# An encoder block on one core: five of the eight column groups of the gate projections by seven half-sized block products, in a stage of their own behind the local attention

## The chip, the cores and the metric

The kernel runs on one core of one Trainium2 chip. The metric is the device time in microseconds (us) of one execution; lower is better. Engines are named as the profile names them: PE (TensorE matmul), PEld (its weight load), DVE (VectorE), ACT (ScalarE), POOL (GpSimd), SP (SyncE, which issues nearly all DMAs here, in order, each after the waits that it carries).

## The reference

One layer of an encoder with 512 tokens and width 2048, all in float32:

```python
mod = silu(c) @ w_ada + b_ada                      # shift, scale, gate for both halves
h   = rms_norm(x) * (1 + sc1) + sh1
qa, ka, va, qb, kb, vb, ga, gb = split(h @ w_in)   # ga, gb: 2048 columns each
ya  = global_gqa(rope(norm(qa)), rope(norm(ka)), va)   # 8 heads, all 512 keys
yb  = neighbourhood_attention(qb, kb, vb, nat_rpb)     # 8 heads, 8x16 windows
m   = sigmoid(ga) * (ya @ w_oa) + sigmoid(gb) * (yb @ w_ob)
x   = x + g1 * (m @ w_out)
h2  = rms_norm(x) * (1 + sc2) + sh2
x   = x + g2 * ((silu(h2 @ w_ffn_gate) * (h2 @ w_ffn_up)) @ w_ffn_down)
out = rms_norm(x)
```

## The kernel before

Every product is made of three float32r matmuls (`mm3`): each operand is split into a high part (ACT copy, `whi`, `..h`) and a low part (DVE or POOL subtraction, `wlo`, `..l`), and high*high, high*low and low*high are summed in PSUM. Weights come in units of 512 KB by SP into the tile `raw` (four buffers), are split into `whi` and `wlo` (three buffers each), and are used once.

Two forms of product are used for the projections. `form1` makes two tiles of 128 output columns over the 16 tiles of the width, tokens along the free axis: 16 x 2 x 3 = 96 matmuls of 512 columns. `form2` makes 512 output columns with tokens on the partitions: 192 such matmuls. In the feed-forward part `group7` makes 512 columns by seven block products of a 2 x 2 blocking (Winograd's variant of Strassen's scheme): for each of four steps over the width, `wforms` loads two units, forms the sums of weight blocks `ta` (DVE) and `tb` (POOL) and splits four tiles; then each of seven products takes 12 matmuls of 256 columns, 84 a step, 336 a group. `xforms` does the same once for the moving operand. Seven DVE additions (lines 765 to 771) put the products together at the end of a group. There the pools have five buffers of `raw` and of the split weights.

The stages, in the order of the program:

1. The first 228 us: norm of x, the modulation `ada1`, h (`hT`, 16 pairs of tiles that stay in SBUF until the gates are done), k and v, the first half of q, the first four column tiles of `ga`.
2. Global attention (`att_a`): four heads, the second half of q (`form2`), `ga` 4 to 8 (`gates`, two `form1`), four heads, `ga` 8 to 16 (four `form1`).
3. Local attention, two halves of four heads: v of the half by `form2` straight into its split tiles (line 572), then twice q and k of two heads (`form1`) and `att_b` for both.
4. `gb` 0 to 16: eight `form1`, each result copied and stored to DRAM (`keep_gate`).
5. The 16 attention results `y_d` are read back (`yr`, in the buffers of `raw`) and split into `yT`; then `w_oa`, `w_ob` with the gates read back; then `w_out`; then the feed-forward part.

Beside the stages runs a queue `bg` of generators, one step of which (`pump`) is taken after each unit of weights: `ada_mod` (eight generators, the second modulation) from stage 3 on, then `ada_gate` (eight generators, two gate rows); a step loads 512 KB of `w_ada` into a `raw` buffer and adds it up with two DVE instructions (line 257).

A scheduler puts each engine's instructions in a fixed order: it follows the program, but moves work of a later statement ahead where an earlier one still waits and buffers are free. So the matmuls of the next `form1` or `form2` stand among those of the heads. A pool that is released and allocated anew sets a limit to this: what lies in the new one waits for what lay there before. The weight pools `wp` and `io` live from the start to the end of `w_ob`.

Of the kernel before, what the change touches and what calls it, by code (L numbers as in the profile page):

```python
# [80 lines left out]
def encoder_block(ctx: ExitStack, tc, xp, c, w_ada, b_ada, norm1_w, w_in, q_norm_w, k_norm_w, tb,  # L81
# [197 lines left out]
    def ada_gate(col, q, dst):  # L279
# [6 lines left out]
        y = bank("Y")  # L286
# [111 lines left out]
    def keep_gate(dst):  # L398
        def evac(w, j, b):
            o = io.tile([P, T], F32, tag="go", name="go", bufs=2)  # L400
# [104 lines left out]
    for h in range(4):  # L505
        att_a(h, q, h, 0)
    q1 = [st(F32) for _ in range(NT)]
# [9 lines left out]
    gates(sg_a, GA, 8, 16, G)  # L517
# [62 lines left out]

    bg.extend(ada_gate(2 * D, q, g1_d) for q in range(4))
    bg.extend(ada_gate(5 * D, q, g2_d) for q in range(4))
    gates(sg_b, GB, 0, KT)
    p_b.release()
    p_h.release()

# [89 lines left out]
    ORDER = (1, 2, 3, 5, 6, 7, 4)  # L676
    HALVES = ((1,), (2, 3), (5, 6), (7, 4)), ((1,), (2, 4), (5, 6), (7, 3))
    BANK = {1: "mm", 2: "mm", 3: "mm", 5: "mm", 6: "S", 7: "S", 4: "Y"}

    def form_pool(name, side):  # L680
        return tc.alloc_tile_pool(name=name, bufs=1, side=side, reuse_waits="tile")

    def half(t, n=2):
        return t.rearrange("p (a q n) -> p a q n", q=2, n=256) if n == 2 else t.rearrange("p (q n) -> p q n", q=2)

    def split7(parts, tiles, kinds):

        d = {}
        for (src, views), (hi, lo), rs in zip(parts, tiles, kinds):
            split(hi, lo, src)  # L690
            for r, v in zip(rs, views):
                d[r] = (v(hi), v(lo))
        return d

    def wforms(w, k0, c0):
        rt = []
        for a in range(2):
            raw, r3 = unit(w, k0 + 2 * a, 2, c0, 512)
            rt.append((raw, r3[:, :, :256], r3[:, :, 256:]))
        (_, b11, b12), (r1, b21, b22) = rt  # L700
        ta = wp.tile([P, 1024], F32, tag="ta", name="ta", bufs=2)
        tb = wp.tile([P, 1024], F32, tag="tb", name="tb", bufs=1)
        t1, t2_ = (half(ta)[:, a] for a in range(2))
        t3, t4 = (half(tb)[:, a] for a in range(2))
        V.tensor_sub(t1, b12, b11)
        V.tensor_sub(t2_, b22, t1)
        G.tensor_sub(t3, b22, b12)  # L707
        G.tensor_sub(t4, t2_, b21)  # L708
        hl = [[wtile(t) for t in ("whi", "wlo")] for _ in range(4)]
        col = lambda e: lambda t: t.rearrange("p (q n) -> p q n", q=2)[:, :, e * 256:(e + 1) * 256]  # L710
        blk = lambda e: lambda t: half(t)[:, e]
        g0 = [t[:, :512].rearrange("p (q n) -> p q n", q=2) for t in hl[0]]
        return split7(((b11, (lambda t: t,)), (r1, (col(0), col(1))), (ta, (blk(0), blk(1))), (tb, (blk(0), blk(1)))),
                      [g0] + hl[1:], HALVES[0])

    def xforms(pool, e, o, full=False):

        sa = wp.tile([P, 1024], F32, tag="ta", name="sa", bufs=2)
        sb = wp.tile([P, 1024], F32, tag="tb", name="sb", bufs=1)
        a11, a21 = e[:, :512], e[:, 512:]  # L720
        a12, a22 = o[:, :512], o[:, 512:]
        V.tensor_add(sa[:, :512], a21, a22)
        V.tensor_sub(sa[:, 512:], sa[:, :512], a11)
        G.tensor_sub(sb[:, :512], a11, a21)
        G.tensor_sub(sb[:, 512:], a12, sa[:, 512:])
        tl = [[pool.tile([P, 512 if n == 0 else 1024], F32R, tag=f"x{n}{t}", name=f"x{n}{t}") for t in "hl"]
              for n in range(4)]
        blk = lambda n: lambda t: t[:, n * 512:(n + 1) * 512].rearrange("p (q n) -> p q n", q=2)
        d = {}
        if full:  # L730
            h21 = [wtile(t)[:, :512] for t in ("whi", "wlo")]
            split(*tl[0], a11)
            split(*h21, a21)
            split(*tl[1], o)
            d["21"] = tuple(blk(0)(t) for t in h21)
            for n, rs in ((0, (1,)), (1, (2, 4))):
                for j, r in enumerate(rs):
                    d[r] = tuple(blk(j)(t) for t in tl[n])
            d.update(split7(((sa, (blk(0), blk(1))), (sb, (blk(0), blk(1)))), tl[2:], HALVES[1][2:]))
            return d  # L740
        return split7(((a11, (blk(0),)), (o, (blk(0), blk(1))), (sa, (blk(0), blk(1))), (sb, (blk(0), blk(1)))),
                      tl, HALVES[1])

    at7 = iter((4, 8, 12, 16, 20, 24, 28, 32, 36, 40, 44, 48, 52, 56, 60, 0, 1, 2, 56, 24, 40))

    def group7(wsrc, xs, order, dst):

        wbufs["at"] = next(at7)
        bk = {r: bank(BANK[r]) for r in ORDER}
        for n, s in enumerate(order):  # L750
            w = wsrc(s)
            for r in ORDER:
                (wh, wl), (xh, xl) = w[r], xs[s][r]
                for q in range(2):
                    for c in range(2):
                        o = bk[r][:, c * 256:(c + 1) * 256]
                        cs = slice(c * P, (c + 1) * P)
                        first, last = n == 0 and q == 0 and c == 0, n == len(order) - 1 and q == 1
                        mm3(o, wh[:, q, cs], wl[:, q, cs], xh[:, q], xl[:, q], first, last, skip_group_check=True)
        p = {r: b.rearrange("p (c n) -> p c n", c=2) for r, b in bk.items()}  # L760
        (d11, d12), (d21, d22) = dst
        with tc.high_priority():
            p1 = io.tile([P, 512], F32, tag="io", name="p1").rearrange("p (c n) -> p c n", c=2)
            S.activation(p1, p[1], AF.Copy)
            V.tensor_add(d11, p[2], p1)
            V.tensor_add(d21, p[6], p1)
            V.tensor_add(d12, p[5], d21)
            V.tensor_add(d12, p[3], d12)
            V.tensor_add(d21, p[7], d21)
            V.tensor_add(d22, p[5], d21)  # L770
            V.tensor_sub(d21, d21, p[4])

# [188 lines left out]
```

## Time and profile before

| | |
|---|---|
| median of 3 runs | 2812.9 us (2806.91, 2812.9, 2821.86) |
| span of the profiled execution | 2800.4 us (its own time is not listed apart) |
| PE busy | 2672.3 us, 95% of the span |
| DVE, ACT, POOL busy | 1730.4, 961.7, 617.0 us |
| moved by DMA | 427.17 MB, mean 153 GB/s |
| global attention and what stands beside it | about 228 to 497 us |
| local attention | about 497 to 818 us |
| `gb` | from about 793 us, beside the last two heads, to 986 us |
| `w_oa` and `w_ob`, `w_out` | 992 to 1171 us, 1175 to 1368 us |
| feed-forward, first part (21 `group7`) and second part | to about 2285 us, to 2800 us |

"Span" runs from the first to the last instruction; a run's time has some us more around it. Busy shares of PE are modelled, so the distance between the starts of two matmuls says more on its pace than the busy time.

### The profile page before, as it was taken

How to read it: one execution, taken by the hardware profiler on the slowest of the kernel's cores; microseconds unless marked ns; L12 is line 12 of the kernel's file. 1: busy time of each engine (PE TensorE's matmuls, PEld its weight loads, DVE VectorE, ACT ScalarE, POOL GpSimd, SP SyncE). 2: the span in 40 equal slices, each digit the busy share in tenths (PEclk: the TensorE clock that was granted, in tenths of full speed). 3: DMA queues.
4: the chain of work that ended last, by engine and by line, in shares of the span. 5: the costliest groups of instructions: out<-in, count | busy, mean ns of one | idle time of the engine just before them, and what ended most of it. 6: DMA issues, size and time to landing. Idle time of an engine off the chain costs nothing.

```text
span 2800.4 us, 38853 instructions
## 1 busy us (share of the span) xinstructions
PE 2672.3 (95%) x15353; PEld 2331.3 (83%) x15353; DVE 1730.4 (62%) x2277; ACT 961.7 (34%) x1310; POOL 617.0 (22%) x366
## 2 busy tenths in 40 slices
PE   5888999999999999899899999999999989999998
PEld 4676878788887878677789999999999988878886
DVE  8987461566665566565568877777788753243227
ACT  4224441233331233222544444444444433122122
POOL 2544323000100000011123443333434410011000
PEclk8889999999999999999989999999999999999999
DMA  8772224655556577676333343334333354343232
GB/s 256 255 235 83 83 68 153 193 157 168 173 168 198 186 254 249 221 260 199 95 113 121 122 128 118 116 108 130 126 119 120 125 192 163 97 143 120 90 113 83
DMA packets 281238, 427.17 MB, mean 153 GB/s; under 512 B 16992, under 2 KB 148432, under 8 KB 278496
## 3 DMA queue, kind: packets, MB, share of 16 engines
q1 hardware_dynamic: 280720, 423.59, 46.9%
q8 instruction: 120, 1.97, 0.3%
q10 hardware_dynamic: 336, 1.11, 0.1%
q14 instruction: 62, 0.51, 0.1%
HBM read 392.11 MB, written 32.52 MB: 152 GB/s over the span
## 4 chain that ended last, share of the span: by engine, by line
PE 77%; DVE 10%; DMA 8%; ACT 2%; issue 2%; SPq 0%; POOL 0%; DVEq 0%; ACTq 0%
PE mm L122 19%; PE mm L124 19%; PE mm L123 19%; DMA raw<-in_w_ada 6%; DVE acc L257 5%; PE S L122 3%; PE S L123 3%; PE S L124 3%; PE Y L122 2%; PE Y L123 2%; PE Y L124 2%; DMA ffr<-ffd 1%; ACT whi L114 1%; PE T L494 1%; DVE wlo L115 0%
## 5 line engine op out<-in xcount | busy, mean ns | idle before, releaser
L114 ACT ACTIVATE whi<-raw 128x1024 fp32r<-128x1024 f32 (+1 forms) x466 | 455.2, 978 | 1077.0 <-PE mm L124 404.8
L115 DVE TENSOR_TENSOR wlo<-raw,whi 128x1024 fp32r<-128x1024 f32 (+1 forms) x408 | 499.4, 1227 | 494.6 <-ACT whi L114 489.7
L257 DVE SCALAR_TENSOR_TENSOR acc<-raw,cact,acc 128x512 f32<-128x512 f32 (+1 forms) x383 | 324.9, 851 | 138.0 <-DMA raw<-in_w_ada 129.0
L707 POOL TENSOR_TENSOR tb<-raw 128x512 f32<-128x512 f32 x84 | 116.0, 1380 | 505.6 <-DVE wlo L115 497.8
L115 POOL TENSOR_TENSOR wlo<-raw,whi 128x1024 fp32r<-128x1024 f32 (+1 forms) x58 | 142.7, 2465 | 236.5 <-ACT whi L114 204.9
L115 DVE TENSOR_TENSOR wlo<-ta,whi 128x1024 fp32r<-128x1024 f32 x84 | 129.4, 1541 | 70.5 <-ACT whi L114 70.1
L708 POOL TENSOR_TENSOR tb<-ta,raw 128x512 f32<-128x512 f32 x84 | 145.1, 1727 | 0.0
L646 POOL TENSOR_TENSOR xr<-xr,ro 128x512 f32<-128x512 f32 x32 | 49.3, 1572 | 434.0 <-DVE ro L645 434.0
L114 ACT ACTIVATE whi<-ta 128x1024 fp32r<-128x1024 f32 x84 | 89.2, 1062 | 142.1 <-PE mm L123 142.1
L114 ACT ACTIVATE whi<-tb 128x1024 fp32r<-128x1024 f32 x84 | 89.1, 1061 | 133.4 <-PE S L123 119.9
L123 PE MATMUL mm<-x1l,whi 128*128 128x256 f32 x400 | 112.4, 281 | 0.0
L122 PE MATMUL mm<-x1h,whi 128*128 128x256 f32 x400 | 112.3, 281 | 0.0
L124 PE MATMUL mm<-x1h,wlo 128*128 128x256 f32 x400 | 112.3, 281 | 0.0
L115 DVE TENSOR_TENSOR wlo<-tb,whi 128x1024 fp32r<-128x1024 f32 x84 | 102.5, 1221 | 10.0 <-ACT whi L114 8.3
L122 PE MATMUL mm<-x0h,whi 128*128 128x256 f32 x368 | 104.5, 285 | 3.3 <-ACT whi L114 3.3
L124 PE MATMUL mm<-x0h,wlo 128*128 128x256 f32 x368 | 104.4, 284 | 0.8 <-DVE wlo L115 0.8
L123 PE MATMUL mm<-x0l,whi 128*128 128x256 f32 x368 | 104.5, 284 | 0.0
L250 POOL MEMSET acc<- 128x512 f32 x8 | 4.2, 526 | 427.9 <-DVE ada_s L115 158.6
L123 PE MATMUL mm<-x3l,whi 128*128 128x256 f32 x336 | 94.3, 281 | 0.0
L123 PE MATMUL S<-x2l,whi 128*128 128x256 f32 x336 | 94.3, 281 | 0.0
L123 PE MATMUL S<-x3l,whi 128*128 128x256 f32 x336 | 94.3, 281 | 0.0
L123 PE MATMUL mm<-x2l,whi 128*128 128x256 f32 x336 | 94.3, 281 | 0.0
(1311 smaller groups left out, 8242.9 us busy)
## 6 DMA issues: line engine op xcount, KB each, us to landing
raw<-in_w_in SPq DMA_DIRECT2D x134, 512.0 KB
raw<-in_w_ada SPq DMA_DIRECT2D x256, 256.0 KB
raw<-in_w_gate SPq DMA_DIRECT2D x88, 512.0 KB
raw<-in_w_up SPq DMA_DIRECT2D x88, 512.0 KB
raw<-in_w_down SPq DMA_DIRECT2D x88, 512.0 KB
raw<-in_w_ada SPq DMA_DIRECT2D x64, 512.0 KB
raw<-in_w_out SPq DMA_DIRECT2D x40, 512.0 KB
ffr<-ffd SPq DMA_DIRECT2D x22, 512.0 KB
```

The costliest lines, as they stand in the source:

```text
L114: S.activation(hi, src, AF.Copy)
L115: eng.tensor_sub(lo, src, hi)
L122: nc.tensor.matmul(o, lh, rh, start=start, stop=False, **kw)
L123: nc.tensor.matmul(o, lh, rl, start=False, stop=False, **kw)
L124: nc.tensor.matmul(o, ll, rh, start=False, stop=stop, **kw)
L250: G.memset(acc, 0.0)
L257: V.scalar_tensor_tensor(acc, part, cact[:, k:k + 1], acc, op0=ALU.mult, op1=ALU.add)
L494: nc.tensor.transpose(tp[:, k * P:(k + 1) * P], e[:, k * P:(k + 1) * P], ident)
L646: eng.tensor_add(x2[i][:, cs], x2[i][:, cs], o)
L707: G.tensor_sub(t3, b22, b12)
L708: G.tensor_sub(t4, t2_, b21)
```

## The change

- `ada_mod` joins the queue already behind the first four heads of the global attention; it was ahead of the local attention.
- `ga` 8 to 16 leave their place behind the global attention. There v of both halves of the local attention is made now (`form2`), copied from PSUM and stored to DRAM (`vbd`); at the start of each half it is read back (`vr`, in the buffers of `raw`) and split.
- Behind the last head all that is left of `bg` is run to its end (`settle`); `p_b`, `io` and `wp` are released, and a stage of its own begins with pools `wg`, `iog` (`raw` four buffers, split weights three) and `p_s`. It makes `gb` 0 to 4 by two pairs of `form1` as before. Beside them `hforms` forms the sums of blocks of h (POOL adds high and low part into `eo`, in buffers of `raw`; DVE forms `sa`, `sb`; 8 splits in all). Three of the seven products need no new tile: a small class `Block` hands out slices of `hT`.
- Then five `group7` of 512 columns: `gb` 4 to 16 and `ga` 8 to 16, results by way of the tile `c` to DRAM. `group7` takes a `pump` per step now. `ada_gate` runs in this stage and goes on in `w_oa`; its small product lies in bank "T" instead of "Y".
- At the end one `settle`, release of the four pools, new pools `wo` and `ioo`, and the code from `gpool` on as before. The definitions of `group7`, `wforms` and the rest are moved ahead, unchanged.

```diff
+    def settle():
+        if bg:
+            for _ in bg.pop(0):
+                pass
...
     for h in range(4):
         att_a(h, q, h, 0)
+    bg.extend(ada_mod(3 * D, 4 * D, k, 2, (s2, b_sc2, n2, t2, b_sh2)) for k in range(0, KT, 2))
...
-    gates(sg_a, GA, 8, 16, G)
+    vb_d = [[dram.tile([P, T], F32, name=f"vbd{h}{i}") for i in range(NT)] for h in range(2)]
+    for h in range(2):
+        form2(w_in, VB + h * 512, hT, lambda i, b: keep_gate(vb_d[h])(0, i, b), eng=G)
...
-    bg.extend(ada_mod(3 * D, 4 * D, k, 2, (s2, b_sc2, n2, t2, b_sh2)) for k in range(0, KT, 2))
     for half in range(2):
         v = [pair(p_b, "v", 512, NT) for _ in range(NT)]
-        form2(w_in, VB + half * 512, hT, lambda i, b: split(*v[i], b))
+        for i in range(NT):
+            vr = wp.tile([P, 1024], F32, tag="raw", name="vr", bufs=4)[:, :512]
+            nc.sync.dma_start(vr, vb_d[half][i])
+            split(*v[i], vr)
...
-    bg.extend(ada_gate(2 * D, q, g1_d) for q in range(4))
-    bg.extend(ada_gate(5 * D, q, g2_d) for q in range(4))
-    gates(sg_b, GB, 0, KT)
+    while bg:
+        settle()
     p_b.release()
+    io.release()
+    wp.release()
...
+    wp = tc.alloc_tile_pool(name="wg", bufs=1, side="right", reuse_waits="tile")
+    io = tc.alloc_tile_pool(name="iog", bufs=3, side="right", reuse_waits="tile")
+    bg.extend(ada_gate(2 * D, q, g1_d) for q in range(4))
+    bg.extend(ada_gate(5 * D, q, g2_d) for q in range(4))
+    p_s = form_pool("p_s", "right")
...
+    def hforms(s):
+        eo = []
+        for a in range(2):
+            r = wp.tile([P, 1024], F32, tag="raw", name="eo", bufs=wbufs["raw"])
+            for q in range(2):
+                hi, lo = (t.rearrange("p (t n) -> p t n", t=2) for t in hT[4 * s + 2 * a + q])
+                G.tensor_add(half(r)[:, :, q], hi, lo)
+            eo.append(r)
+        (a11, a21), (a12, a22) = ((r[:, :512], r[:, 512:]) for r in eo)
+        sa = wp.tile([P, 1024], F32, tag="ta", name="sa", bufs=2)
+        sb = wp.tile([P, 1024], F32, tag="tb", name="sb", bufs=1)
+        V.tensor_add(sa[:, :512], a21, a22)
+        V.tensor_sub(sa[:, 512:], sa[:, :512], a11)
+        V.tensor_sub(sb[:, :512], a11, a21)
+        V.tensor_sub(sb[:, 512:], a12, sa[:, 512:])
...
+    for j in range(0, 4, 2):
+        form1([w_in], GB + j * P, 2, hT, [[bank("mm"), bank("mm")]], keep_gate(sg_b[j:], "io", 3))
+        gx += [hforms(j), hforms(j + 1)]
+    for base, dst, j0, j1 in ((GB, sg_b, 4, KT), (GA, sg_a, 8, KT)):
+        for j in range(j0, j1, 4):
+            c = io.tile([P, 2048], F32, tag="c", name="c", bufs=1)
...
+            group7(lambda s: wforms(w_in, 4 * s, base + j * P), gx, range(4),
+                   ((v[:, 0, 0], v[:, 1, 0]), (v[:, 0, 1], v[:, 1, 1])), 16)
...
+    settle()
+    p_s.release()
+    io.release()
+    wp.release()
     p_h.release()
+    wp = tc.alloc_tile_pool(name="wo", bufs=1, side="right", reuse_waits="tile")
+    io = tc.alloc_tile_pool(name="ioo", bufs=3, side="right", reuse_waits="tile")
```

Three places show how the order of instructions moves. In the rows, a name left of the arrow is written, names right of it are read; `mm`, `S`, `T`, `Y` are PSUM banks; line numbers after the change are higher by some lines.

PE before, at the first scores of heads 2 and 3 of the local attention (`S<-qk..`); `mm<-whi,h0h` is the next dense product, v of the second half:

```order
L124 MATMUL mm<-h15h,wlo 128x512
L122 MATMUL mm<-whi,h0h 128x512
L122 MATMUL S<-qkh 128x256
L122 MATMUL S<-qkh 128x384
L123 MATMUL mm<-wlo,h0h 128x512
L124 MATMUL mm<-whi,h0l 128x512
L123 MATMUL S<-qkl,qkh 128x256
L124 MATMUL S<-qkh,qkl 128x256
L123 MATMUL S<-qkl,qkh 128x384
L124 MATMUL S<-qkh,qkl 128x384
```

PE now, from the last part of the same two heads (`T<-ident,e` transposes, `Y<-pt..` the weighted sums) to the first dense product behind them, q of the second half:

```order
L124 MATMUL Y<-pth,vl 128x256
L564 MATMUL T<-ident,e 128x128 x8
L122 MATMUL Y<-pth,vh 128x384
L564 MATMUL T<-ident,e 128x128 x2
L123 MATMUL Y<-ptl,vh 128x384
L124 MATMUL Y<-pth,vl 128x384
L122 MATMUL Y<-pth,vh 128x256
L123 MATMUL Y<-ptl,vh 128x256
L124 MATMUL Y<-pth,vl 128x256
L122 MATMUL mm<-h0h,whi 128x512
```

From the first scores of heads 2 and 3 to their last sum no `mm` row stands on PE any more; the same holds for heads 6 and 7.

SP now, around the reading back of v for the second half (`vr`), ahead of the weights of q (`raw<-in_w_in`); `y_1975`, `y_1976` are the results of heads 2 and 3, `braw` the tables of the bias:

```order
L471 DMA y_1974<-yo 128x512
L581 DMA vr<-vbd_3593 128x512
L539 DMA braw<-in_tb 8x720 x16
L581 DMA vr<-vbd_3594 128x512
L581 DMA vr<-vbd_3595 128x512
L581 DMA vr<-vbd_3596 128x512
L539 DMA braw<-in_tb 8x720 x16
L471 DMA y_1975<-yo 128x512
L539 DMA braw<-in_tb 8x720 x4
L129 DMA raw<-in_w_in 128x4x256
L471 DMA y_1976<-yo 128x512
```

The four `vr` hold all four `raw` buffers; the first weights of q behind them wait until DVE has split the first, which in turn waits for the last sums of head 3, since the tiles of v are the same ones.

SP before, where the attention results are read back (`yr<-y`), ahead of the last stores of `gb` (`sgb_427`, `sgb_428`, its last two tiles):

```order
L597 DMA yr<-y_1965 128x512
L597 DMA yr<-y_1966 128x512
L402 DMA sgb_425<-go 128x512
L597 DMA yr<-y_1967 128x512
L402 DMA sgb_426<-go 128x512
L597 DMA yr<-y_1968 128x512
...
L597 DMA yr<-y_1980 128x512
L129 DMA raw<-in_w_oa 128x4x256 x2
L242 DMA raw<-in_w_ada 128x2x512
L129 DMA raw<-in_w_ob 128x4x256
L402 DMA sgb_427<-go 128x512
```

SP now, at the same place; `sga_411` to `sga_410` are the results of the last `group7`, `gate<-g1d` waits for PE's last read of `hT`:

```order
L247 DMA raw<-in_w_ada 128x2x512 x5
L301 DMA gate_9331<-g1d_4202 128x512
L764 DMA yr<-y_1965 128x512
L764 DMA yr<-y_1966 128x512
L764 DMA yr<-y_1967 128x512
L744 DMA sga_411<-c 256x1x256
...
L744 DMA sga_410<-c 256x1x256
L296 DMA g1d_4205<-ada_o 1x512
L764 DMA yr<-y_1968 128x512
...
L764 DMA yr<-y_1980 128x512
L301 DMA gate_9331<-g1d_4204 128x512
L129 DMA raw<-in_w_oa 128x4x256
```

Before, all 16 results are read back ahead of the stores of the last two tiles of `gb`. Now 13 of the 16 stand behind the results of the last `group7`, and the first weights of `w_oa` behind all 16.

More of the change, by code (lines that the diff above doesn't have):

```diff
@@ L285, in ada_gate @@
         split(hi, lo, acc)
-        y = bank("Y")
+        y = bank("T")
         nc.tensor.matmul(y, ones_r, hi, start=True, stop=False)
@@ L396, in encoder_block, with keep_gate @@
     p_x.release()
-    def keep_gate(dst):
+    def keep_gate(dst, tag="go", bufs=2):
         def evac(w, j, b):
-            o = io.tile([P, T], F32, tag="go", name="go", bufs=2)
+            o = io.tile([P, T], F32, tag=tag, name="go", bufs=bufs)
             V.tensor_copy(o, b)
@@ L671, in encoder_block @@
     gpool.release()
[L676 to L742, printed above, removed]
@@ L744, in encoder_block @@
-    at7 = iter((4, 8, 12, 16, 20, 24, 28, 32, 36, 40, 44, 48, 52, 56, 60, 0, 1, 2, 56, 24, 40))
[L746 to L771, printed above, removed]
@@ L834, in encoder_block @@
             dst = (v[:, 0, 0], v[:, 1, 0]), (v[:, 0, 1], v[:, 1, 1])
-            group7(lambda s: wforms(w, 4 * s, n * 512), hx, range(SU), dst)
+            group7(lambda s: wforms(w, 4 * s, n * 512), hx, range(SU), dst, next(at7))
             if w is w_gate:
```

108 lines of the change are left out of this document (107 added, 1 removed).

## The prediction

> **What bounds the kernel now.** I read the page first, then the busy time by stage, then the starts of single matmuls.
>
> ```profile
> span 2800.4 us, 38853 instructions
> PE 2672.3 (95%) x15353; PEld 2331.3 (83%) x15353; DVE 1730.4 (62%) x2277; ACT 961.7 (34%) x1310; POOL 617.0 (22%) x366
> 820.00:997.00 177.00, 168.97 (x730) 138.30 (x729) 92.26 (x116) 41.98 (x47) 1.52 (x3) 0.97 0.63 199
> 1620.00:1740.00 120.00, 120.00 (x1008) 120.00 (x1008) 94.18 (x93) 48.93 (x53) 47.64 (x28) 1.00 0.37 119
> ```
>
> Behind the stretch and its length stand the busy times of PE, PEld, DVE, ACT and POOL, then the granted clock, the DMA share and GB/s. PE bounds nearly everywhere: in the gates (820 to 997) and in the feed-forward block products (1620 to 1740), which run without a stall. DVE is busy there 94.18 of 120 us, so it has 21% left.
>
> **What a block product is worth.** In order of start, duration:
>
> ```profile
> 825.78 0.39 PE L122 MATMUL mm<-h0h,whi 128*128 128x512 f32 x1
> ...
> 847.54 0.39 PE L122 MATMUL mm<-h0h,whi 128*128 128x512 f32 x1
> 1692.21 0.28 PE L122 MATMUL S<-x3h,whi 128*128 128x256 f32 x1
> ...
> 1702.29 0.29 PE L122 MATMUL S<-x3h,whi 128*128 128x256 f32 x1
> ```
>
> The first two rows are the starts of two neighbouring `form1`: 96 matmuls of 512 columns in 21.76 us, 227 ns each. The other two are one step of `group7` apart: 84 matmuls of 256 columns in 10.08 us, 120 ns each. So half the columns cost 53% of the time. A group costs 2 x 21.76 = 43.5 us before and 4 x 10.08 = 40.3 now: five groups save 16 us on PE, not the eighth of 218 us (27) that counting columns gives. The Trainium skill (TensorE: Matmul & The Clock Gate, Back-to-back issue gap) gives N/2.4 + 2.5 ns for a warm matmul; estimated from it a group falls from 41.4 to 36.7 us, the five save 24 and the sum below would be 8 us lower. The rows here differ (227 and 120 ns against 216 and 109), so they decide.
>
> **Term 1, heads 2 and 3 without cover: +11.** In the new order PE has no dense product between the first scores and the last sum of these heads. Before, such a pair ran like this (start and end; stretch; then DVE over all four pairs of the stage, count, busy, mean ns):
>
> ```profile
> 792.80 0.51 PE L122 MATMUL S<-qkh 128*128 128x256 f32 x2
> ...
> 817.65 0.28 PE L124 MATMUL Y<-pth,vl 128*128 128x256 f32 x1
> 792.80:818.00 25.20, 25.20 (x134) 20.60 (x134) 22.21 (x59) 11.80 (x30) 0.00 (x0) 1.00 0.44 134
> L115 DVE TENSOR_TENSOR ptl<-T,pth 128x256 fp32r<-128x256 f32 (+1 forms) x32 | 15.6, 488 | 4.7 <-ACT pth L114 4.4
> L552 DVE SCALAR_TENSOR_TENSOR sb<-S,bm 128x256 f32<-128x256 f32 (+1 forms) x32 | 15.1, 479 | 0.1
> L471 DVE TENSOR_REDUCE mx<-sb 128x1 f32<-128x256 f32 (+1 forms) x32 | 14.8, 471 | 0.1
> L478 DVE TENSOR_SCALAR e<-e,rs 128x256 f32<-128x256 f32 (+1 forms) x32 | 12.7, 402 | 0.0
> L477 DVE RECIPROCAL rs<-sm 128x1 f32<-128x1 f32 x32 | 4.8, 155 | 0.6 <-ACT e L475 0.5
> L472 DVE TENSOR_SCALAR mx<-mx 128x1 f32<-128x1 f32 x32 | 4.6, 145 | 0.1
> L257 DVE SCALAR_TENSOR_TENSOR acc<-raw,cact,acc 128x512 f32<-128x512 f32 x83 | 63.5, 765 | 31.7 <-DMA raw<-in_w_ada 30.5
> ```
>
> PE was full for all 25 us. The pair's own part of it is 48 products of 256 or 384 columns at 0.12 to 0.17 us and 20 transposes at most as long as a 256: about 9 us. What remains alone is a chain over DVE: 67.6 / 4 = 16.9 us a pair by these rows, and the way through ACT and PE for the first and last block. Bounds of the chain: 13 us if durations overlap by a fifth, 25 as before. I take 20, nearer the DVE rows: PE idles 20 - 9 = 11 (4 to 16).
>
> **Term 2, v read back: +9.** Then q of the second half waits for a split of v (0.6 on ACT and 0.69 on DVE for 128x512), a transfer of 512 KB and a split of the weights. The nearest rows are the crossing from the gates to `w_oa`:
>
> ```profile
> 986.20 0.39 PE L124 MATMUL mm<-h15h,wlo 128*128 128x512 f32 x1
> 991.60 0.54 PE L122 MATMUL mm<-y0h,whi 128*128 128x512 f32 x1 [5.01 <-issue]
> 995.42 0.39 PE L124 MATMUL mm<-y1h,wlo 128*128 128x512 f32 x1
> 985.50 4.83 DMA raw<-in_w_oa
> 990.44 1.06 ACT whi L114
> 992.00:996.00 4.00, 3.76 (x11) 2.58 (x10) 3.08 (x4) 2.09 (x2) 0.00 (x0) 0.59 0.81 297
> L114 ACT ACTIVATE vh<-mm x8: 598/598/600, 536.0 to 694.2; 128x512 fp32r<-128x512 f32 x8
> L115 DVE TENSOR_TENSOR vl<-mm,vh x8: 679/686/692, 537.6 to 694.8; 128x512 fp32r<-128x512 f32 x8
> ```
>
> 4.83 us of transfer and 1.06 us of split stand ahead of the first matmul; behind it nine took 3.8 us where 2.0 would do, at a granted clock of 0.59: +1.8. So 1.3 + 4.8 + 1.1 + 1.8 = 9 (6 to 11, with or without the slow start and a prefetch).
>
> **Term 3, heads 6 and 7 without cover: +16.** As term 1, but `settle` puts ten of `ada_mod`'s DVE additions among the heads (0.77 us each in the last row of term 1, some waiting for their transfer behind the 16 of `braw`): 5 us more than term 1 (8 to 25).
>
> **Term 4, start of the gates' own stage: +9.** The first weights of `gb` stand on SP behind the store of head 7's result, so nothing is prefetched: copy 0.6, transfer 4.8, split 1.1, slow start 1.8 (6 to 12).
>
> **Term 5, end of that stage: +26.** Before, the 16 `yr` ran beside the last gates:
>
> ```profile
> 969.02 15.89 SPq L597 DMA_DIRECT2D yr<-y  x13
> L768 DVE TENSOR_TENSOR c<-mm,c 128x512 f32<-128x512 f32 x21 | 14.5, 691 | 0.7
> L115 DVE TENSOR_TENSOR wlo<-raw,whi 128x1024 fp32r<-128x1024 f32 (+1 forms) x408 | 499.4, 1227 | 494.6 <-ACT whi L114 489.7
> L257 DVE SCALAR_TENSOR_TENSOR acc<-raw,cact,acc 128x512 f32<-128x512 f32 (+1 forms) x383 | 324.9, 851 | 138.0 <-DMA raw<-in_w_ada 129.0
> 818.59 2.77 DMA y<-yo
> ```
>
> 13 issues in 15.89 us, 1.22 us each, paced by four buffers. Now they begin when PE is done with `hT`, and their splits when `c` is stored. From PE's last matmul: copy and seven additions 0.6 + 7 x 0.69 = 5.4; some of the last `ada_gate` additions between them, 3; store 2.8; four splits 2.8; nine more `yr` until a buffer is free for `w_oa`, 11; transfer and split 5.9. That is 31 us, less the 5.4 us of the same gap before (986.20 to 991.60): +26 (19, if splits don't wait for the store, to 35).
>
> **Term 6, DVE in the new stage: +5.** A step needs 94.18 / 120 x 10.08 = 7.9 us of DVE as in the feed-forward part, and two additions of `ada_gate`, 1.7: 9.6 of 10.08. With three buffers of split weights instead of five a late DVE stops PE soon. `hforms` (16 operations of 0.7, 8 splits of 1.2) beside two `form1` pairs, 16 additions and 8 splits comes to about 46 us of DVE in 43.5. I take 1 us a group (0 to 20 for all).
>
> **At nothing.** The cover of what moves ahead is the full PE of the global attention:
>
> ```profile
> 228.00:342.00 114.00, 102.84 (x511) 82.53 (x510) 71.86 (x158) 48.44 (x114) 39.74 (x22) 0.96 0.23 73
> 342.00:402.00 60.00, 56.24 (x282) 44.13 (x281) 33.32 (x72) 22.95 (x41) 20.18 (x10) 1.00 0.29 92
> ```
>
> v instead of `ga` 8 to 16 beside heads 4 to 7: 2 x 192 matmuls for 4 x 96. Eight copies, stores, reads and splits more: 0.7 us each on DVE beside a full PE; uncovered they would cost 6. `ada_mod` moved ahead: 128 additions beside the global attention, where DVE was busy 63% and 56% and the DMA share 0.23 and 0.29; where it delays a head's chain, up to 10. `ada_gate` leaving `w_out` may give back 2.
>
> **Sum**: -16 + 11 + 9 + 16 + 9 + 26 + 5 = +60 on the span of 2800.4 us. The runs lie 6 to 21 us above that span, the median 12.5; so 2812.9 + 60 = 2873.
>
> A stretch like the two uncovered pairs has one near relation, the crossing into the feed-forward part, with PE 72% busy:
>
> ```profile
> 1370.00:1425.00 55.00, 39.61 (x264) 36.05 (x265) 34.40 (x46) 35.67 (x47) 12.63 (x8) 0.79 0.20 64
> ```
>
> The granted clock is 0.79 there. At half clock the pair's products would lengthen each block's chain by some 0.6 us, 5 us a pair: 2883, inside the forecast. The same page of the Trainium skill (Part 1: The HAM clock gate) states half clock after an idle window of about 3.4 us, which this row neither excludes nor shows for matmuls spread thinly.
>
> **Rivals.**
> - *The crossings are covered after all*: pools with tile-wise waits let weights come early and the heads' chains run at 13 us. For it: PE's gap at 986 was only 5.4 us. Against: SP's order holds `raw` behind the last store in all three. Terms 1 to 5 then take their lower ends, 4 + 6 + 8 + 6 + 19: +27 with no stall in the new stage, 2840.
> - *DVE becomes the bound of the new stage*: POOL beside it and waits for `w_ada` make a step 11 us. 20 steps at 0.9 more, and 5 for the forms, make 23 to 25 instead of 5: 2893. The point is 10.08 us; 9.6 by the rows speaks slightly against.
> - *Faster, the block products alone decide*: the uncovered stretches come to little, since PE needs no cover that the heads' other engines don't bound: -16, 2797. It decides where terms 1 to 6 stay under 16 us together; term 5 alone exceeds that by the rows.
> - *No effect*: the stretches cost about what the products save, 2815.
>
> **How the numbers follow.** Two measurements of this kernel can be told apart from about 0.5%, 14 us. Chances: forecast (2850 to 2885) 0.58, covered crossings 0.17, DVE bound 0.12, faster 0.07, no effect 0.06. Slower is the sum of the first three, 0.87; same 0.06; faster 0.07. The range goes from the covered case less what the lowest run lies under the median (2840 - 6) to a bound DVE with what the highest lies above it (2893 + 9); it leaves out the last two and the tails.
>
> **What would show it.** Term 1 and 3: two stretches near 25 us of local attention with PE half idle and no `mm` row. Terms 2 and 4: PE waits of 6 to 8 us for `whi`, ended by a transfer of `w_in`. Term 5: a PE gap near 30 us ahead of the first `y0h` matmul. Term 6: steps of `group7` over 10.08 us, waits of PE for `wlo`. The saving: 120 ns between starts in the new stage. I am wrong if these gaps are absent, or if the steps are far from 10.08 us.

## The result and the profile after

The changed kernel takes 2920.5 us (median of 4 runs, 2913.7 to 2923.8) against 2811.4 for the kernel before on the same chip: ratio 1.0389, 95% interval [1.0374, 1.0405]. It is slower, as forecast, but 47 us beyond the forecast of 2873 and 18 above the upper end of the range, 2902. The profiled execution took 2913.7 us, its span is 2911.9: 111.5 more than before.

First lines of the page after:

```profile
span 2911.9 us, 40705 instructions
PE 2688.9 (92%) x16073; PEld 2365.9 (81%) x16073; DVE 1865.7 (64%) x2404; ACT 1008.1 (35%) x1363; POOL 706.2 (24%) x422
```

PE's busy time grew by 17 us, the span by 111.5: most of the time is in waits. Busy time by stretch (columns as in the prediction), of heads 2 and 3, of heads 6 and 7, of the last four `group7`, and of the piece from `ga` 4 to 8 to the local attention (first after the change, then before it):

```profile
616.00:642.00 26.00, 19.24 (x69) 14.60 (x68) 17.55 (x52) 10.80 (x29) 2.43 (x3) 0.59 0.05 14
752.80:777.50 24.70, 14.86 (x69) 10.75 (x68) 22.00 (x60) 9.50 (x26) 0.00 (x0) 0.86 0.10 33
895.50:1075.50 180.00, 164.26 (x1350) 159.60 (x1348) 151.02 (x161) 62.18 (x68) 49.02 (x31) 0.98 0.53 164
366.10:516.60 150.50, 132.09 (x631) 104.93 (x629) 82.17 (x154) 44.83 (x77) 39.84 (x19) 0.95 0.48 149
365.10:491.40 126.30, 121.80 (x607) 98.00 (x606) 58.47 (x118) 42.55 (x73) 38.85 (x19) 1.00 0.36 116
```

The two stretches of heads, in which PE was full before, have it at 19 of 26 and 15 of 25 us, the first at a granted clock of 0.59, the second at 0.86. In the last two rows 384 dense products of 512 columns stand beside heads 4 to 7 each time; after the change PE is idle there for 18.4 us instead of 4.5.

The matmuls that bound the pieces (start, duration; in brackets PE's idle time before and what ended it): first v product and first score of head 4; first q product of the local attention; both crossings between its halves; starts of the first, second and last `group7`; the end of the stage. The second and third row are DVE's, ahead of that first score: an addition of `ada_mod` that waits for its transfer, and `ql`, for which PE then waits.

```profile
366.08 0.48 PE L122 MATMUL mm<-whi,h0h 128*128 128x512 f32 x1
370.13 1.54 DVE L262 SCALAR_TENSOR_TENSOR acc<-raw,cact,acc 128x512 f32<-128x512 f32 x2 [5.67 <-DMA raw<-in_w_ada]
373.45 0.68 DVE L115 TENSOR_TENSOR ql<-T,qh 128x512 fp32r<-128x512 f32 x1
374.19 0.79 PE L124 MATMUL S<-kh,ql 128*128 128x512 f32 x1 [5.87 <-DVE ql L115]
516.60 0.63 PE L122 MATMUL mm<-h0h,whi 128*128 128x512 f32 x1
616.05 0.56 PE L122 MATMUL S<-qkh 128*128 128x256 f32 x2
645.82 0.79 PE L122 MATMUL mm<-h0h,whi 128*128 128x512 f32 x1 [3.46 <-ACT whi L114]
697.87 0.39 PE L122 MATMUL mm<-h0h,whi 128*128 128x512 f32 x1
752.84 0.56 PE L122 MATMUL S<-qkh 128*128 128x256 f32 x2
785.35 0.79 PE L122 MATMUL mm<-h0h,whi 128*128 128x512 f32 x1 [4.90 <-ACT whi L114]
840.77 0.39 PE L122 MATMUL mm<-h0h,whi 128*128 128x256 f32 x1 [2.48 <-ACT whi L114]
895.53 0.28 PE L122 MATMUL mm<-h0h,whi 128*128 128x256 f32 x1
...
1031.54 0.28 PE L122 MATMUL mm<-h0h,whi 128*128 128x256 f32 x1
1075.45 0.28 PE L124 MATMUL Y<-h15h,wlo 128*128 128x256 f32 x1
1107.89 0.76 PE L122 MATMUL mm<-y0h,whi 128*128 128x512 f32 x1 [27.14 <-ACT whi L114]
```

The groups take 54.8 us (the first) and 44 to 46 (the others, 180.2 in all) where 40.3 was the pace; before them the two `form1` take 55.4 where 43.5 was. What DVE waits for in the last four groups (total us, times, longest), and where the chain that ended last spends that stretch:

```profile
DVE acc L262 <- DMA raw<-in_w_ada: 14.7, 8, 2.7
DVE ta L627 <- DMA raw<-in_w_in: 12.5, 9, 4.1
by line: DVE wlo L115 18.7%; issue 16.3%; DMA raw<-in_w_in 13.7%; DMA raw<-in_w_ada 12.1%; DVE acc L262 8.6%; PE mm L124 3.2%; PE mm L122 2.7%; PE mm L123 2.6%; DVE ta L626 2.3%; POOL tb L628 1.6%; DVE ta L627 1.6%; DVE c L688 1.5%; DVE c L
```

This is the reading that counts. PE is "busy" 164 of 180 us and DVE 151, but DVE's busy time and its waits for transfers make 151 + 27 = 178: in its fixed order DVE has next to nothing left. The chain runs over DVE's splits, the buffer that a split frees and the transfer into it; PE's products into `mm` have 8.5% of it.

### The profile page after: what moved, and what is told of

Its sections match the earlier page's. It is cut to its first block, busy times and chain, and to the rows that moved or that the text cites. A ratio compares the mean times of both kernels' runs of the same rounds, so it can differ in the third digit from the quotient of the medians.

```text
span 2911.9 us, 40705 instructions
## 1 busy us (share of the span) xinstructions
PE 2688.9 (92%) x16073; PEld 2365.9 (81%) x16073; DVE 1865.7 (64%) x2404; ACT 1008.1 (35%) x1363; POOL 706.2 (24%) x422
## 4 chain that ended last, share of the span: by engine, by line
PE 64%; DVE 14%; DMA 10%; issue 8%; ACT 2%; POOL 2%; SPq 0%; DVEq 0%; ACTq 0%; POOLq 0%
PE mm L124 16%; PE mm L123 16%; PE mm L122 16%; DVE acc L262 6%; DMA raw<-in_w_ada 4%; PE S L122 3%; PE S L124 3%; PE S L123 3%; DMA raw<-in_w_in 2%; DVE wlo L115 2%; PE Y L122 2%; PE Y L123 2%; PE Y L124 2%; POOL wlo L115 1%; DMA ffr<-ffd 1%
## 5 line engine op out<-in xcount | busy, mean ns | idle before, releaser
L115 DVE TENSOR_TENSOR wlo<-raw,whi 128x1024 fp32r<-128x1024 f32 (+1 forms) x408 | 506.3, 1244 | 517.8 <-ACT whi L114 515.7
L114 ACT ACTIVATE whi<-raw 128x1024 fp32r<-128x1024 f32 (+1 forms) x466 | 447.1, 960 | 1010.0 <-PE mm L124 383.0
L262 DVE SCALAR_TENSOR_TENSOR acc<-raw,cact,acc 128x512 f32<-128x512 f32 (+1 forms) x383 | 338.2, 885 | 117.0 <-DMA raw<-in_w_ada 110.7
L628 POOL TENSOR_TENSOR tb<-raw 128x512 f32<-128x512 f32 x104 | 148.4, 1427 | 661.0 <-DVE wlo L115 644.9
L115 DVE TENSOR_TENSOR wlo<-ta,whi 128x1024 fp32r<-128x1024 f32 x104 | 153.9, 1480 | 71.5 <-ACT whi L114 71.1
L629 POOL TENSOR_TENSOR tb<-ta,raw 128x512 f32<-128x512 f32 x104 | 178.5, 1716 | 0.1
L114 ACT ACTIVATE whi<-ta 128x1024 fp32r<-128x1024 f32 x104 | 110.4, 1062 | 176.3 <-PE mm L123 142.4
L114 ACT ACTIVATE whi<-tb 128x1024 fp32r<-128x1024 f32 x104 | 110.4, 1061 | 143.4 <-PE S L123 119.9
L115 DVE TENSOR_TENSOR wlo<-tb,whi 128x1024 fp32r<-128x1024 f32 x104 | 126.9, 1220 | 9.8 <-ACT whi L114 8.2
L626 DVE TENSOR_TENSOR ta<-raw 128x512 f32<-128x512 f32 x104 | 98.3, 945 | 8.7 <-DMA raw<-in_w_in 0.9
```

The source lines that it names most:

```text
L114: S.activation(hi, src, AF.Copy)
L115: eng.tensor_sub(lo, src, hi)
L262: V.scalar_tensor_tensor(acc, part, cact[:, k:k + 1], acc, op0=ALU.mult, op1=ALU.add)
```

## The experiments

The code up to `ga` 4 to 8 is the same in nearly all of them, and in the profiled executions it ended anywhere from 365 to 379 us. So pieces are compared by their own length, totals by medians (before: 2808 to 2812 beside each call; after: 2920.5).

**No `ada_gate` in the new stage.**

```diff
-    bg.extend(ada_gate(...)) for both gates    # ahead of hforms
-    settle()                                   # behind the last group7
+    bg.extend(ada_gate(...)) for both gates    # ahead of w_oa
+    settle()                                   # ahead of w_out
```

> The eight sums of `ada_gate` leave the new gates stage and run beside `w_oa` and `w_out`; all else as after the change. Theory A (DVE stands in order behind additions whose w_ada transfer is late, and PE then lacks `wlo`): the five `group7` fall from 235 us to 203 to 210, the two `form1` pairs with `hforms` from 57 to about 50, and w_out takes back its 5 to 6 us; total about 2890. Theory B (the 16 splits and sums of a group are too much for DVE, ACT and POOL as they are): the groups stay within 1 us of 45 each, total 2914 to 2926.

2888.5 us, ratio to before 1.0277 [1.0261, 1.0292]. Start of the stage, start of the first group, the last block product, the first `w_oa` product, then the window over the five groups and the chain over the last four:

```profile
784.08 0.79 PE L122 MATMUL mm<-h0h,whi 128*128 128x512 f32 x1 [4.96 <-ACT whi L114]
834.59 0.28 PE L122 MATMUL mm<-h0h,whi 128*128 128x256 f32 x1
...
1033.59 0.28 PE L124 MATMUL Y<-h15h,wlo 128*128 128x256 f32 x1
1060.18 0.77 PE L122 MATMUL mm<-y0h,whi 128*128 128x512 f32 x1 [26.30 <-DMA raw<-in_w_ada]
834.60:1033.60 199.00, 197.02 (x1681) 196.47 (x1679) 162.12 (x152) 77.08 (x83) 58.44 (x39) 1.00 0.40 120
by line: PE mm L122 18.7%; PE mm L124 18.4%; PE mm L123 18.4%; PE S L122 9.3%; PE S L124 9.2%; PE S L123 9.2%; PE Y L122 4.5%; PE Y L124 4.5%; PE Y L123 4.5%; DVE c L689 0.9%; issue 0.8%; DVE c L687 0.4%; DVE c L688 0.4%; DVE c L691 0.4%; D
```

Five groups in 199 us instead of 235, PE full and the chain on PE's own products: theory A. DVE still waits, but now for ACT's copies (23.4 of its 30 us of waits in the last four groups), which wait for buffers that PE frees. The two `form1` with `hforms` fell from 55.4 to 50.5 and the end of the stage from 32.4 to 26.6. From the first `w_oa` product to the first product of the feed-forward part it is 17.1 us longer (400.3 against 383.3), not 5 to 6; a gap of 11 us stands where `settle` runs ahead of `w_out`.

**Additions without their transfers.** They all read one tile that was loaded once:

```diff
+            if "z" in wbufs and nj == 1:
+                yield [(k0 + e, wbufs["z"][:, e * 512:(e + 1) * 512]) for e in range(nk)]
+                continue
```

> As after the change, but in the new gates stage the additions of `ada_gate` all read one tile that was loaded once, so that their transfers fall away while their DVE time stays (the first gate vector, and the part of the second that is summed in this stage, are then not those of the reference). Theory A (DVE is held by late transfers of w_ada on top of its work): DVE keeps 1.65 us of additions a step and loses its waits for w_ada, a group falls from 45 to 41 to 42.5 us, total 2898 to 2908. Theory B (the additions' own time is too much for DVE): groups stay above 44, total 2915 to 2923. Theory C (the transfers disturb everything): as without any `ada_gate`, 39.6 to 40.3, total 2888 to 2893.

2909.4 us. DVE's work on `acc` in the first four groups: the stretch from the start of a group to that of the next, then busy time and count:

```profile
858.25:912.74 54.49, 21.06 (x27) 0.87 0.34 100
912.74:953.91 41.17, 6.39 (x8) 1.00 0.41 127
953.91:1000.50 46.59, 14.81 (x16) 1.00 0.39 114
1000.50:1040.03 39.53, 0.68 (x1) 1.00 0.46 136
```

With nothing to wait for, about the same work (43.6 us in the five groups, 42.4 after the change) stands elsewhere: 27, 8, 16, 1 and 1 instructions on `acc`, where after the change it is 9, 9, 6, 8 and 17. The mean of the last four groups, 41.5 us, lies in theory A's range, but the groups behind it are not alike. The second group, with eight, takes 41.2 us, against 44.8 to 45.8 for the second to fourth after the change, with six to nine and their transfers, and 39.7 without `ada_gate`: at an even pace most of the loss goes with the transfers. The third, with 16, takes 46.6, and the first, with 27 and what is left of `hforms`, 54.5, against 40.2 without `ada_gate`: there the additions' own time on DVE is enough. The count alone does not set it, since the last group after the change has 17 and takes 44.0. Over all five groups 14 of the 36 us lost go with the transfers and 22 stay. So theory A holds in part, and theory B where additions bunch; the total is 1 us above theory A's bounds.

**More buffers** in the new stage:

```diff
-    wbufs.update(pad=64)
+    wbufs.update(pad=64, raw=6, w=4)
```

> The new stage gets six `raw` and four pairs of split weights instead of four and three; the sums of `ada_gate` stay in it. Theory A (DVE stands behind transfers that go out too late for want of buffers): the five `group7` fall from 235 us to 205 to 215, total 2895 to 2905. Theory B (the sums' own DVE time and their place in DVE's order make the wait, whenever the transfer goes out): the groups stay above 43.5 us each, total 2912 to 2922.

2912.0 us [1.0333, 1.0388]; the five groups 232.8 us (850.59 to 1083.37). DVE's longest waits, from the second group on:

```profile
DVE acc L262 <- DMA raw<-in_w_ada: 21.7, 10, 4.9
```

The waits for `w_in` went, those for `w_ada` grew from 14.7 to 21.7. So buffers do not cure it: the times are theory B's. What holds the transfers then is open. SP, which stands in order, waited in that stretch 47.0 us for buffers that DVE's splits free and 21.2 for `c` ahead of its stores; neither wait was taken away.

**Plain `form1` in the new stage**, everything else in place:

```diff
-    group7(...) for gb 4 to 16, ga 8 to 16; hforms
+    form1([w_in], base + j * P, 2, hT, ...) for the same columns
```

> The new gates stage with plain `form1` in place of the five `group7` and without `hforms`; place, pools and order of everything else as after the change. Theory A (the block products as fed here cost more than their columns save): twelve `form1` pairs at 21.8 us, 261 us and up to 10 of stalls in place of 292; total 2890 to 2900. Theory B (the stage is slow by its place and pools, not by the block products): the stage stays near 290 us or grows by the 16 us of columns, total 2920 to 2937.

2889.7 us [1.0261, 1.0301]: theory A. Start of the first `form1`, and the last matmul:

```profile
792.03 0.80 PE L122 MATMUL mm<-h0h,whi 128*128 128x512 f32 x1 [3.52 <-ACT whi L114]
...
1059.70 0.39 PE L124 MATMUL mm<-h15h,wlo 128*128 128x512 f32 x1
```

Twelve forms take 268 us with the additions beside them, 7 over their pace of 261; with block products the same columns took 290 (785.35 to 1075.7). Without additions (first experiment, 784.08 to 1033.8) two `form1` and the block products need 250. So beside `ada_gate` the block products lose 22 us to plain forms. Their saving without it was not measured alike on both sides: it is 18 against the forms with the additions beside them, and 11 against the forms at their pace, since `hforms` still cost 7. The totals of the two runs are the same (2889.7 and 2888.5), as the additions cost their price elsewhere. A `form1` leaves DVE the room, a `group7` doesn't.

**`ada_mod` back at its old place**, v stays ahead:

```diff
-    bg.extend(ada_mod(...))      # ahead of q of heads 4 to 7
+    bg.extend(ada_mod(...))      # ahead of the local attention
```

> The sums of `ada_mod` start where they did before the change (behind v), v itself stays ahead. Theory A (the moved sums delay heads 4 to 7 and the v products): the stretch from the end of `ga` 4 to 8 to the first q product of the local attention falls from 150.5 to about 130 us; the heads 0 to 7 of the local attention get up to 6 us longer; total 2903 to 2910. Theory B (v's copies, stores and POOL splits are what is slow): the stretch stays at 145 to 150, total 2918 to 2930.

The first v product, the first q product of the local attention, and what PE waited for between 764 and 806 us, behind head 7 (total, times, longest):

```profile
366.55 0.48 PE L122 MATMUL mm<-whi,h0h 128*128 128x512 f32 x1
495.05 0.47 PE L122 MATMUL mm<-h0h,whi 128*128 128x512 f32 x1 [0.78 <-DVE go L406]
PE Y L280 <- DVE acc L262: 25.2, 2, 12.8
```

The stretch is 128.5 us instead of 150.5 (theory A), within 2 of before. But the total rose to 2938.9: with v and the gates gone from the places where a step of the queue is taken, three generators were left over, and `settle` ran them behind head 7 with nothing beside, 12 to 13 us each (the third ends at 806.25). That consequence the expectation did not have.

**The same move alone, in the kernel before:**

```diff
+    bg.extend(ada_mod(...))      # ahead of q of heads 4 to 7
-    bg.extend(ada_mod(...))      # ahead of the local attention
```

> The kernel before the change with one thing moved: the sums of `ada_mod` start ahead of q of heads 4 to 7 instead of ahead of the local attention. Theory A (these sums beside the global attention delay its chains by themselves): heads 4 to 7 and `ga` 8 to 15 behind them take 15 to 22 us longer, up to 8 come back in the gates, whose stalls go; total 2817 to 2830. Theory B (they cost only together with v's copies and splits): total 2802 to 2814.

2829.1 us, ratio 1.0070 [1.0051, 1.0089]: a small loss, in theory A's range. Heads 4 to 7 with four `form1` of `ga` up to the first v product, here:

```profile
370.97 0.47 PE L122 MATMUL mm<-h0h,whi 128*128 128x512 f32 x1
524.83 0.39 PE L122 MATMUL mm<-whi,h0h 128*128 128x512 f32 x1
```

That is 153.9 us; before the change the same rows stand at 365.11 and 491.40, 126.3. The sums cost 27.6 there with no copy of v in sight, and 10 came back up to `w_oa` (570.50 to 1013.54, against 538.31 to 991.60 before).

**Both halves of v read back ahead of the heads:**

```diff
+    for half in range(2):
+        v = [pair(p_b, "v", 512, 2 * NT) for _ in range(NT)]
+        ...                       # read and split, as before
     for half in range(2):
-        v = [pair(p_b, "v", 512, NT) for _ in range(NT)]
-        ...
```

> Both halves of v are read back and split ahead of the first head into twice the buffers, so nothing stands between the heads 0 to 3 and q of the second half. Theory A (the order and buffers of v are what uncovers heads 2 and 3): q of the second half runs beside them, their 29.8 us of stretch and reload and the slow two `form1` behind shrink by 20 to 27; total 2893 to 2901. Theory B (the cover fails for another reason, the q and k buffers or the weights): PE still stands between the heads 2 and 3, gain under 8 us, total above 2912.

2904.8 us [1.0319, 1.0366]. The first q product, then q of the second half and the first score of head 2:

```profile
531.08 0.80 PE L122 MATMUL mm<-h0h,whi 128*128 128x512 f32 x1 [11.83 <-ACT whi L114]
635.61 0.39 PE L122 MATMUL mm<-h0h,whi 128*128 128x512 f32 x1
635.84 0.51 PE L122 MATMUL S<-qkh 128*128 128x256 f32 x2
```

Now q of the second half starts with the first score of head 2 and covers it. From the first q product to the gates it is 247.1 us instead of 268.8, 21.7 less, as theory A says. Eight reads ahead of the first q product took 8 back, so the total fell by 16 where 20 to 27 was expected.

**Both `gb` pairs of `form1` beside heads 6 and 7:**

```diff
+    for j in range(0, 4, 2):
+        form1([w_in], GB + j * P, 2, hT, [[bank("mm"), bank("mm")]], keep_gate(sg_b[j:]))
     while bg:
         settle()
     p_b.release()
...
-        form1(...)                # the same two pairs, in the new stage
```

> The two `form1` pairs of `gb` 0 to 3 are written behind the last head but ahead of the release of the heads' pools, in the old buffers; `hforms` stays in the new stage, now without cover. Theory A (heads 6 and 7 are alone because the stage of the gates starts only after the release): the two pairs run beside them, PE's 30.7 us from the first score of head 6 to the first product of `gb` shrink by about 20, and 5 to 12 us of `hforms` come to stand alone; total 2905 to 2913. Theory B (the `hforms` of all four parts are exposed, 21 us of DVE): the two cancel, total 2917 to 2925.

2921.8 us: theory B. The heads were covered, but the first block product waited:

```profile
848.75 0.58 PE L122 MATMUL mm<-h0h,whi 128*128 128x256 f32 x1 [33.74 <-ACT whi L114]
820.42 1.73 DVE L723 TENSOR_TENSOR sa<-eo 128x512 f32<-128x512 f32 x1 [4.08 <-POOL eo L718]
845.67 0.68 DVE L723 TENSOR_TENSOR sa<-eo 128x512 f32<-128x512 f32 x1
831.67 2.24 POOL L718 TENSOR_TENSOR eo<-h11h,h11l 128x512 f32<-128x512 f32 x1
```

The first weights stand behind eight `eo` in the buffers of `raw`, and for 34 us only `hforms` runs. The cover that `hforms` had in the new stage was worth what the uncovered heads cost.

**Eight own buffers for `yr`, waits tile by tile:**

```diff
-    p_y = tc.alloc_tile_pool(name="p_y", bufs=1, side="right")
+    p_y = tc.alloc_tile_pool(name="p_y", bufs=1, side="right", reuse_waits="tile")
-        yr = wp.tile([P, 1024], F32, tag="raw", name="yr", bufs=4)[:, :T]
+        yr = p_y.tile([P, T], F32, tag="yr", name="yr", bufs=8)
```

> `yr` gets eight buffers of its own (instead of four of `raw`), and the pool of `yT` waits tile by tile; all else as after the change. Theory A (the 32 us between the last `group7` and the first `w_oa` product come from the pool's one wait for the stores of `c` and from 16 reads through four buffers): that gap falls to 18 to 24 us, total 2907 to 2913. Theory B (the sums of `c` and their stores on SP's order set it): the gap stays over 28 us, total 2916 to 2924.

Last block product and first `w_oa` product:

```profile
1084.51 0.28 PE L124 MATMUL Y<-h15h,wlo 128*128 128x256 f32 x1
1100.88 1.22 PE L122 MATMUL mm<-y0h,whi 128*128 128x512 f32 x2 [11.06 <-ACT y0h L114]
```

The gap is 16.4 us instead of 32.4, below theory A's bounds. The median, 2918.0 (2913 to 2922), hardly shows it: `w_oa` and `w_out` took 9 back (392.5 us from 1100.88 to the first product of the feed-forward part, against 383.3), and the profiled execution reached the first v product 7 us later than that of after.

**All repairs together**, as the expectation lists them. What the edits above do not have yet:

```diff
+    bg.extend(...)                # all 16 generators, ahead of the v products; acc in a pool that stays
-    while bg: settle()            # ahead of p_b.release()
-            pump()                # in group7
+            if s not in xs:                      # in group7, for s = 2, 3
+                xs[s] = hforms(s)
+        pump()                    # twice for each pair of w_oa columns
```

> All repairs together: v of each half in buffers of its own, read back one pair of heads early; no additions in the new stage (all of `ada_gate` and `ada_mod` spread over v, q and k, `w_oa` and `w_out`, from the v products on); the first `gb` pair beside heads 6 and 7, the second with two `hforms` in the new stage, the other two `hforms` inside the first `group7`; eight buffers for `yr`. If the terms found so far add up: 18 us saved by the block products against 5 to 8 for v, 5 for the start of the stage, 5 to 10 for `hforms`, 11 for its end, and 0 to 10 for the additions put elsewhere: total 2805 to 2830. If the additions cost as much wherever they stand: 2840 to 2870.

2862.7 us, ratio 1.0188 [1.0156, 1.0221]. Starts of the first two groups, the last block product, the first `w_oa` product, then the window of `w_oa` here and in the kernel before:

```profile
790.53 0.28 PE L123 MATMUL mm<-h0h,whi 128*128 128x256 f32 x1
848.61 0.28 PE L123 MATMUL mm<-h0h,whi 128*128 128x256 f32 x1
...
1005.74 0.28 PE L125 MATMUL Y<-h15h,wlo 128*128 128x256 f32 x1
1018.30 1.22 PE L123 MATMUL mm<-y0h,whi 128*128 128x512 f32 x2 [12.28 <-ACT y0h L115]
1020.00:1230.00 210.00, 189.78 (x806) 154.96 (x805) 145.31 (x208) 70.34 (x92) 0.53 (x1) 0.94 0.76 243
992.00:1175.00 183.00, 177.75 (x776) 145.97 (x774) 122.33 (x161) 64.00 (x84) 1.58 (x3) 0.99 0.71 226
```

The repairs held where they were made: last four groups 39.3 us each, end of the stage 12.6, and from the first q product to the first gate product (504.70 to 715.95) 211.3 us against 210.8 before, v's 43.5 taken off. But `w_oa`, which now took 48 steps of the queue instead of 32, went from 184 to 212, `w_out` from 198 after the change to 211, and the first group with `hforms` took 58. On the spans of the two profiled executions the pieces from the first v product to the first `w_oa` product fell by 93 us against the kernel after the change, and `w_oa` and `w_out` took 39 of them back. The total lies in the second range, "if the additions cost as much wherever they stand". From the first q product of the local attention to the end of the gates the repaired kernel takes 501 us, where the same number of columns took 495 before (491.40 to 986.20, with v in place of `ga` 8 to 16), so the saving of the block products is still used up there; but the largest loss left is `w_oa`, 28 us. The last run asks how much of that goes with the 16 steps.

**Four `hforms` in the first group**, against the run with all repairs:

```diff
-    form1(gb 2, 3) and hforms(0), hforms(1) in the new stage
+    form1(gb 2, 3) ahead of p_b.release(); hforms(s) in group7 for all s
```

> As the run with all repairs, but both `gb` pairs stand beside heads 6 and 7 and all four `hforms` inside the first `group7`. If `hforms` within a step costs only what DVE is over (5 us a step): 10 to 15 us more in the first group and 4 less at the start, within 10 us of that run. If POOL's and DVE's sums slow each other as in the 34 us stretch: 15 to 25 us longer than it.

2870.6 us [1.0185, 1.0244], 8 more: the total of the first expectation. The first group grew by 5 us (791.26 to 854.61), not by 10 to 15.

**The 16 extra steps ahead of heads 4 to 7**, against the run with all repairs:

```diff
+    bg.extend(...)                # all 16 generators, ahead of q of heads 4 to 7
-        pump()                    # twice for each pair of w_oa columns
```

> As the run with all repairs (2863), but the 16 sums that were doubled up beside `w_oa` start 16 places earlier, beside q of heads 4 to 7 and `ga` 4 to 7. Theory A (what a sum costs depends on its place: about 28 us for the 16 beside `w_oa`, 0.3 to 0.9 us each beside the global attention): `w_oa` falls from 212 to about 184 us, the stretch up to the first q product of the local attention grows by 5 to 14; total 2842 to 2856. Theory B (a sum costs the same wherever it stands): total 2859 to 2867.

2865.6 us [1.0164, 1.0211]: theory B's total. `w_oa` fell by 12 us, to 200, and the stretches up to the second `form1` of the local attention grew by 9.5. Why `w_oa` stays 16 above before with its old 32 steps was not settled. No version beat the kernel before.

## Why the prediction was wrong

Terms as forecast, and as the two traces give them on the span:

| term | forecast | measured | from |
|---|---|---|---|
| saving of the block products | -16 | -16 | 12 forms at 21.76, less 2 forms and 5 x 40.3: the paces, without stalls |
| 1 to 4: crossings of the local attention | +45 | +47 | 516.60 to 785.35, against 538.31 to 792.58 less v (43.5) and plus the heads' own PE work (11.4) |
| 5: end of the stage | +26 | +27 | 32.4 against 5.4 |
| 6: DVE in the new stage | +5 | +45 | 33.5 in five groups, 11.9 in two `form1` |
| at nothing: what moves ahead | 0 | +24 | 366.08 to 516.60 against 126.3 for the same products |
| given back, and other stretches | 0 | -16 | 8.5 of stalls in the old gates, 3.4 beside v, 6.1 in `w_oa` and `w_out`; 2.3 lost ahead of 366 us and in the feed-forward part |

The sum is 111, 51 more than the 60 that were forecast. Of these 40 stand in term 6 and 24 in what was put at nothing; the last line gives 16 back. The 11.4 are what the heads add to a `form1` that runs beside them before (792.58 to 825.78, less 21.76).

**Term 6 is the step that failed first.** Its price, 5 us for a DVE at 9.6 of 10.08 us a step, became 45. DVE's work was priced rightly: 151 us over 180 is 9.4 for each 11.25 us step. What was left out is that a split behind an addition waits for the addition's transfer. Busy time of 9.6 in 10.08 needs every input on time and every addition in its own step; 27 us of waits in 16 steps, 1.7 each, made it 11.25. The run without transfers shows that this is not all: where additions bunch, their own time on DVE stops PE too. The rival "DVE becomes the bound" had this mechanism and a step of 11 us, with a chance of 0.12; it was right of this stage, and set `hforms` too low (5 for what cost 12 and made a first group of 55). The parts that the prediction names for `hforms` and what stands beside it make 44 us of DVE, not 46; measured were 47.3 in 55.4 us. Its sums, put at 0.7 us each, took up to 1.79 beside POOL's.

**"At nothing" is the second.** "The full PE" was taken as cover for `ada_mod`, but PE was 90 and 94% busy there with the heads' chains over DVE running in time. DVE's 63% and 56% are averages, and say little on an engine that works in order: after the change PE waits 5.87 us for `ql` of head 4 alone, since DVE's addition ahead of it waited 5.67 for its transfer, and DVE's waits for `w_ada` in the piece grew from 10 to 45 us. The prediction named the price of losing the cover, "up to 10"; putting the sums back saved 22, moving them alone cost 28. Of the 24 us 14 are PE's idle time; 4 are small products of the moved sums, which stood elsewhere before, and the rest comes at a granted clock of 0.95 instead of 1.00.

**What was right.** The pace of a group without additions is 39.7 us (40.3 forecast); the estimate from the Trainium skill (TensorE: Matmul & The Clock Gate, Back-to-back issue gap), 36.7, worked out from its gap for a matmul by itself, is not reached at a granted clock of 1.00. Terms 1 and 2 measured 27 (616.05 to 645.82 less 11.4, and 8.5 over the pace of the two forms up to 697.87; forecast 20), 3 and 4 21 (752.84 to 785.35 less 11.4; forecast 25): both stand at their places, and the run with both halves of v took 21.7 of the first away. That they sum to 47 for 45 is in part luck, since one was too low and the other too high, and the waits of 6 to 8 us for `whi` came as 3.46 and 4.90 with slow `form1` behind them; the granted clock of 0.59 in the first stretch was an aside of the prediction, outside its sum. Term 5 was right in size; by the run with own buffers, pool and `yr` buffers are 16 of its 27, of which 9 came back behind it.

Both failed steps are one mistake: the 144 steps of the queue (16 generators, nine steps each) were treated as filler. They cost little beside `form1` (7 us in twelve), where DVE has a split every 5.4 us, and the change took forty such places away (12 `form1` of gates became 2, with four steps each), and left 20 beside `group7`, where DVE has no room.

## What to carry over

Judge an in-order engine by its busy time plus its waits for transfers in the stage in question; when the two fill the stage it is the bound, whatever the busiest engine's share says. Waits for what the busiest engine itself frees do not count: without `ada_gate` DVE had those, and PE was the bound. Before a dense stage is thinned out, count what runs beside it and find each piece a new place with room on the engine that does it. A background stream's price belongs to its place, and moving it only helps where the new place has a free engine and free transfers.

## What was not expected of the hardware

DVE and POOL slow each other. In the rows of the run with both `gb` pairs beside the heads, the same 128x512 sum takes 1.73 us on DVE while POOL adds, and 0.68 once POOL is done; POOL's own, 1.26 without DVE, took up to 2.24. The Trainium skill (SBUF — State Buffer, SBUF: two separate sides) says that an operation of DVE with two SBUF inputs and one of GpSimd that reads SBUF hold a common port pair in turn, each for a whole instruction; the rows of DVE agree, since 1.73 is 0.68 and most of a POOL addition. POOL's 2.24 is 0.3 more than 1.26 and one such sum, which no run here explains.
